# Dealing the second half of the forgetting heads' values out over the first score slots

## The chip, the core and the metric

The kernel runs on one core of a Trainium2 chip. The core has five engines that work side by side, each through its own instructions in order: TensorE (PE in the profile) multiplies matrices and writes the results to PSUM, VectorE (DVE), ScalarE (ACT) and GpSimd (POOL) work on vectors, and SyncE (SP) issues most of the DMA transfers. Engines wait for each other by semaphores. The metric is the device time of one execution in microseconds (us); shorter is better.

## The reference

One decoder layer over a sequence of 1024 tokens, width 1024, in float32. What matters here, cut to its core:

```python
h = rmsnorm(x, ln1[l])
z = h @ w_in[l]
ml_qk, ml_v, ml_o, ml_i, ml_f, fx_q, fx_k, fx_v, fx_f = jnp.split(z, splits, axis=-1)
mh = mlstm_chunkwise(mq, mk, mv, ig, lf)          # 4 heads of 128
...
fx_out = forgetting_attention(fq, fk, fv, flf)    # 8 heads of 64, causal softmax
x = x + jnp.concatenate([ml_out, fx_out], axis=-1) @ w_out[l]
x = x + cross_attention(rmsnorm(x, ln_x[l]), rmsnorm(mem, ln_mem[l]), ...)
u = jax.nn.relu(rmsnorm(x, ln2[l]) @ w_ff1[l])
x = x + (u * u) @ w_ff2[l]
return rmsnorm(x, ln_f)
```

The change concerns `fx_v`: the 1024 x 512 values of the eight forgetting heads, which are a product of the normed tokens with 512 columns of `w_in`. The attention's scores, `fq` times `fk` with the decay added, are computed at the same time.

## The kernel before, in words

Every large product is made of three passes, since the operands are split into a high and a low part (`hi`, `lo`): `mm3` (lines 186 to 188) issues the matmuls low by high, high by low and high by high into one PSUM bank. `split` (lines 134 to 138) makes the parts: ScalarE copies the high part, VectorE subtracts it for the low one.

The values come from `token_major` (line 486). It takes the weight in two halves `c` of 256 columns, four heads each; a half is cut from two weight tiles (`wh`, `wl`, three buffers each) and computed in eight tiles of 128 tokens. A tile is eight `mm3`, 24 matmuls of width 256, in a PSUM bank that `mm()` takes in turn from mm, tp, m2, tp. Then `fv_sink` scales and splits the bank (L137, L138) and stores it to `fvd` in device memory (L652).

The scores go by slots. `slot` (line 1031) takes one step at each stage of the attention: VectorE takes the maxima of the score made one slot ago (L741, L744), ScalarE the exponentials of the one before that (L756), GpSimd scales (L767), and PE makes the next score, a pair of matmuls (L734, L735), into one of three `sc` banks. So a score needs the bank of the third score before it, which is free after that score's exponential. Inside a slot, `in_order` pins each engine's instructions behind the ones pinned before. The first 13 slots (`LEAD_`) only make scores; from then on each slot also transposes probabilities (L782) and multiplies them with values (L801), and fills up with work on the memory tokens, whose operand `hm` is loaded from `hmd` (L1094).

Around these first slots stands the end of the last mLSTM head, `ml_head(3)`, a generator called `closing`. Its first part ends with the row factors `c_fac`: PE sums squares and denominators (L217), VectorE and GpSimd make the factors (L609 to L617, the power on GpSimd at L204). Then it is asked for in steps. The first step transposes `c_fac` on PE into an `sc` bank (L249 in `to_row`), stores it to `facd` and loads it back as a row `r_a` (L251, L253). The second forms the first half of the head's output (L628, L629) and loads the row's second half (L625), the third forms the second half. The buffer `r_a` exists once, so the second load waits for the first L628.

What nobody pins, the framework orders itself: it builds the instructions in the order of the code and then lists them for each engine by its own estimate of when they can start, within the data dependencies and the pins. The banks of a tag are handed out in the order of the code, so in both kernels no score of the slots behind the first closing step stands ahead of that step's transpose. Tiles of the values that are not pinned fall between the slots where that list finds room for them.

Of the kernel before, what the change touches and what calls it, by code (L numbers as in the profile page):

```python
# [44 lines left out]
def hybrid_layer(ctx: ExitStack, tc: tile.TileContext, a: dict, out: bass.AP):  # L45
# [56 lines left out]
    def mm():  # L102

        tag = banks[turn[0] % len(banks)]
        turn[0] += 1
        return ps_tile(tag)
# [36 lines left out]
    @contextmanager  # L143
    def in_order(engines=COMPUTE):

        traced = nc.cur_bb.bb.instructions
        last = traced[-1]
        yield
        start = next(k for k in reversed(range(len(traced))) if traced[k] is last) + 1
        for i in traced[start:]:  # L150
            if i.engine not in engines:
                continue
            if i.engine in last_of:
                tc.add_manual_dep(
                    i,
                    last_of[i.engine],
                    mybir.DependencyInfo(mybir.DependencyClass.NoSync, mybir.DependencyReason.DATA),
                    reason="in_order",
                )
            last_of[i.engine] = i.name  # L160
# [8 lines left out]
    def weights(src, n=1024):  # L169
        return weight_parts(weight_load(src, n))  # L170
# [13 lines left out]
    def mm3(ps, w, x, first, last, more=False):  # L184

        nc.tensor.matmul(ps, w[1], x[0], start=first, stop=False, skip_group_check=more)  # L186
        nc.tensor.matmul(ps, w[0], x[1], start=False, stop=False, skip_group_check=more)  # L187
        nc.tensor.matmul(ps, w[0], x[0], start=False, stop=last, skip_group_check=more)  # L188

    def both(pair, f):  # L190
        return f(pair[0]), f(pair[1])
# [283 lines left out]
    def gate_cols():  # L475
        for dst, src in ((gcol, rel), (emc, steps)):
            tps = ov_()
            for j in range(8):
                nc.tensor.transpose(tps[:, j * MLH : (j + 1) * MLH], src[0:MLH, j * P : (j + 1) * P], ident[:MLH, :MLH])
            s.activation(dst.rearrange("p a b -> p (a b)"), tps[:, : 8 * MLH], AF.Copy if dst is gcol else AF.Exp, scale=1.0 if dst is gcol else -1.0)  # L480
        cut = (w4(dt=F32R)[:GW], w4(dt=F32R)[:GW])
        for sign in range(2):
            split(cut[0], cut[1], cum, 1.0 - 2.0 * sign)
            for p_ in range(2):
                load(decay[sign, p_], cut[p_].bitcast(F32))


    def token_major(w_src, sink, cs=(0, 1), between={}):

        for c in cs:  # L490
            ws = [both(weights(w_src[c, i]), lambda t: t.rearrange("p (k c) -> p k c", k=4)) for i in range(2)]
            for t in range(8):
                if t in between:
                    between[t]()
                hf, tt = divmod(t, 4)
                ps = mm()[:, 0:256]
                for k in range(KT):
                    x = both(h[hf], lambda z: z[:, k, tt * P : (tt + 1) * P])
                    mm3(ps, x, both(ws[k // 4], lambda z: z[:, k % 4]), k == 0, k == KT - 1)
                sink(t, c, ps)  # L500

    def conv_silu(n, hi, lo):
        w = weights(a["w_in"][n])
        z = z4()
        g.memset(z[:, 0:3], 0.0)
        for _, hf, ps in proj(w, h, 1):
            v.tensor_tensor(out=z[:, 3 + hf * TH : 3 + hf * TH + TH], in0=ps, in1=row[:, hf * TH : hf * TH + TH], op=ALU.mult)
        y = z4()[:, :T]
        cw = VEC["conv_w"] + 4 * n
        v.tensor_scalar(out=y, in0=z[:, 0:T], scalar1=vec[:, cw : cw + 1], scalar2=vec[:, VEC["conv_b"] + n : VEC["conv_b"] + n + 1], op0=ALU.mult, op1=ALU.add)  # L510
        for j in range(1, 4):
            v.scalar_tensor_tensor(out=y, in0=z[:, j : j + T], scalar=vec[:, cw + j : cw + j + 1], in1=y, op0=ALU.mult, op1=ALU.add)
        t = z[:, 0:T]
        s.activation(t, y, AF.Tanh, scale=0.5)
        v.scalar_tensor_tensor(out=y, in0=t, scalar=1.0, in1=y, op0=ALU.add, op1=ALU.mult)
        split(hi, lo, y, 0.5)
        return y
# [136 lines left out]
    closing = iter(())  # L654
# [20 lines left out]

    banks[:] = ["tp", "m2", "tp", "sc", "mm", "sc", "sc"]
    turn[0] = 0
    token_major(a["w_mv"], mv_sink, (1,), {2: row_first, 4: gate_rows})
    gate_cols()
    banks[:] = ["mm", "tp", "m2", "tp"]  # L680
    with tc.issue_after(last_sum.ins):
# [2 lines left out]
    for hd in range(MLH):  # L684
        closing = ml_head(hd, *ready)
# [27 lines left out]
    def fx_step():  # L713
        if coming:
            dst, src = coming.pop(0)
            load(dst.bitcast(F32), src)
# [88 lines left out]
    def fx_close(hd, hf, ov):  # L805
        if hd % 2 == 0:
            om[hf] = w2("f")
        rng = slice(hd % 2 * FXD, hd % 2 * FXD + FXD)
        t = w2("c")
        s.activation(t[0:FXD], ov[FXD:], AF.Copy)  # L810
        v.tensor_tensor(out=om[hf][rng], in0=ov[0:FXD], in1=t[0:FXD], op=ALU.add)

    def fx_store(hd, hf):
        if hd == FXH - 1:
            t = w4(dt=F32R)
            mix_fx[hf].append((t[:, :TH], t[:, TH:]))
            split(*mix_fx[hf][-1], om[hf])
            return
        hi, lo = w2("y", dt=F32R), om[hf].bitcast(F32R)
        split(hi, lo, om[hf])  # L820

        def store():
            load(mix[hf, 0, :, MLH + hd // 2], hi.bitcast(F32))
            load(mix[hf, 1, :, MLH + hd // 2], lo.bitcast(F32))

        late.append(store)
# [104 lines left out]
    def mix_step():  # L931
        if pieces:
            dst, src = pieces.pop(0)
            load(dst.bitcast(F32), src)
# [65 lines left out]
    def cut_next():  # L1000

        n, e = divmod(halves[0], 2)
        if n < len(sources) and (e or n < len(raws_) and now[1] - ages[n] >= AGE and sum(u >= now[0] for u, _ in sources[:n]) < 3):
            cut_half()
            return True
# [20 lines left out]
    def slot(values, until):  # L1026
        with in_order((*COMPUTE, mybir.EngineType.SP) if values or until else COMPUTE):
            now[1] += 1
            todo_ = late[:]
            late.clear()  # L1030
            closing = bool(ended)
            ended.clear()
            x = next(steps_, None) if values else None
            if x:
                x.turn()

            while adds and not closing and len(adds) >= (LAG if x else 1):
                y = adds.pop(0)
                y.add()
                if y.last:  # L1040
                    ended.append((y.hd, y.hf, y.ov))
                    break
            tops = scored[:]
            scored.clear()
            for t, e in tops:
                t.top(e)
            if x:
                x.cut()
                adds.append(x)
            exps = topped[:]  # L1050
            topped[:] = tops
            for t, e in exps:
                t.exp(e)
            while exped:
                exped.pop(0).scale()
            exped.extend(t for t, e in exps if e == len(t.parts) - 1)
            for hd, hf, ov in ended:
                fx_close(hd, hf, ov)
                if hd % 2:
                    stores.append((hd, hf, True))  # L1060
            fx_step()
            mix_step()
            part = next(parts, None)
            if part:
                part[0].score(part[1])
                scored.append(part)
            late.extend(filter(None, [f() for f in todo_]))
            if stores and stores[0][2]:
                stores[0] = (*stores[0][:2], False)
            elif stores:  # L1070
                fx_store(*stores.pop(0)[:2])
            while spent[0] < until:
                step = next(fill, None)
                if step is None:
                    break
                spent[0] += step[0]
                if step[1]:
                    late.append(step[2])
                    break
            if until and cut_next() and spent[0] + 6 < until:  # L1080
                cut_next()
        return x
# [2 lines left out]
    fx_load(1)  # L1085
    while coming:
        fx_step()
    for i in range(LEAD_):
        slot(False, 0)
        if i in (1, 11):  # L1090
            next(closing, None)
    token_major(a["w_fv"], fv_sink, between={4: lambda: next(closing, None)})
    hm = act().rearrange("p a b -> p (a b)").rearrange("p (e k c) -> p e k c", e=2, k=KT)
    load(hm.bitcast(F32), hmd)  # L1094
    banks[:] = ["mm", "m2"]
# [752 lines left out]
```

## Time and profile before

| what | value |
|---|---|
| median of 3 runs | 1511.72 us |
| lowest, highest | 1510.87, 1512.04 us |
| profiled execution, span | 1509.2 us |
| median less span | 2.5 us |
| granted TensorE clock, mean | 0.997 |
| PE busy | 1493.0 us (99%) |
| VectorE busy | 1122.7 us (74%) |
| ScalarE busy | 757.7 us (50%) |
| GpSimd busy | 528.7 us (35%) |

The span runs from the first to the last instruction of one profiled execution; its time with what lies around it was not listed apart from the runs. In the rows of a timeline stand the start in us, the duration, the engine, the line, the operation, what it writes and reads, and in brackets the idle time of that engine just before and what ended it. A matmul's duration includes its way through the array; the next one starts before it ends, so the pace is read from the starts. In the table by stretches stand the stretch and its length, then for PE, the weight loads, VectorE, ScalarE and GpSimd the busy time and in brackets the instructions, then the granted clock (1.00 is full), the DMA share and GB/s. The stage of the change lies between about 350 and 400 us.

### The profile page before, as it was taken

How to read it: one execution, taken by the hardware profiler on the slowest of the kernel's cores; microseconds unless marked ns; L12 is line 12 of the kernel's file. 1: busy time of each engine (PE TensorE's matmuls, PEld its weight loads, DVE VectorE, ACT ScalarE, POOL GpSimd, SP SyncE). 2: the span in 40 equal slices, each digit the busy share in tenths (PEclk: the TensorE clock that was granted, in tenths of full speed). 3: DMA queues.
4: the chain of work that ended last, by engine and by line, in shares of the span. 5: the costliest groups of instructions: out<-in, count | busy, mean ns of one | idle time of the engine just before them, and what ended most of it. 6: DMA issues, size and time to landing. Idle time of an engine off the chain costs nothing.

```text
span 1509.2 us, 22358 instructions
## 1 busy us (share of the span) xinstructions
PE 1493.0 (99%) x7806; PEld 1263.7 (84%) x7806; DVE 1122.7 (74%) x1803; ACT 757.7 (50%) x1440; POOL 528.7 (35%) x545
## 2 busy tenths in 40 slices
PE   9999999999999999999999999999999999999997
PEld 9988888889899888788988878888888888888887
DVE  7766676664788875667767899989996678787765
ACT  7324343334688764566654467566664521122134
POOL 1003030414365441623300044454544365553312
PEclk9999999999999999999999999999999999999999
DMA  6322333435777877853354447676678677776623
GB/s 243 115 79 95 98 108 126 132 129 153 247 261 256 284 248 246 271 169 126 128 182 159 147 155 279 235 261 248 217 273 292 264 279 279 279 272 251 247 88 112
DMA packets 124276, 303.04 MB, mean 201 GB/s; under 512 B 13810, under 2 KB 28460, under 8 KB 117252
## 3 DMA queue, kind: packets, MB, share of 16 engines
q1 hardware_dynamic: 124164, 301.62, 57.3%
q8 instruction: 61, 1.00, 0.3%
q14 instruction: 51, 0.42, 0.1%
HBM read 202.75 MB, written 98.82 MB: 200 GB/s over the span
## 4 chain that ended last, share of the span: by engine, by line
PE 90%; DMA 4%; DVE 3%; ACT 1%; issue 1%; POOL 1%; POOLq 0%; DVEq 0%; SPq 0%; ACTq 0%
PE tp L186 8%; PE tp L187 8%; PE tp L188 8%; PE sc L186 6%; PE sc L188 6%; PE sc L187 6%; PE mm L186 5%; PE m L188 5%; PE m L186 5%; PE m L187 5%; PE mm L188 5%; PE mm L187 5%; PE ov L801 2%; PE ov L186 2%; PE ov L187 2%; PE ov L188 2%
## 5 line engine op out<-in xcount | busy, mean ns | idle before, releaser
L186 PE MATMUL tp<-act,wl 128*128 128x512 f32 (+1 forms) x440 | 172.6, 392 | 0.0
L187 PE MATMUL tp<-act,wh 128*128 128x512 f32 (+1 forms) x440 | 172.1, 391 | 0.0
L188 PE MATMUL tp<-act,wh 128*128 128x512 f32 (+1 forms) x440 | 171.8, 392 | 0.0
L135 DVE TENSOR_TENSOR wl<-wr,wh 128x1024 fp32r<-128x1024 f32 (+2 forms) x99 | 131.4, 1327 | 27.0 <-ACT wh L134 26.7
L134 ACT ACTIVATE wh<-wr 128x1024 fp32r<-128x1024 f32 (+2 forms) x99 | 99.8, 1008 | 85.7 <-PE tp L188 32.7
L186 PE MATMUL mm<-act,wl 128*128 128x512 f32 (+1 forms) x332 | 124.8, 376 | 2.6 <-DVE r_c L138 2.1
L188 PE MATMUL mm<-act,wh 128*128 128x512 f32 (+1 forms) x332 | 124.1, 374 | 0.0
L187 PE MATMUL mm<-act,wh 128*128 128x512 f32 (+1 forms) x332 | 123.8, 373 | 0.0
L186 PE MATMUL m<-act,wl 128*128 128x512 f32 (+1 forms) x308 | 113.8, 369 | 0.6 <-DVE wl L135 0.6
L188 PE MATMUL m<-act,wh 128*128 128x512 f32 (+1 forms) x308 | 113.8, 369 | 0.0
L187 PE MATMUL m<-act,wh 128*128 128x512 f32 (+1 forms) x308 | 113.7, 369 | 0.0
L188 PE MATMUL sc<-act,wh 128*128 128x512 f32 (+1 forms) x280 | 105.6, 377 | 0.0
L187 PE MATMUL sc<-act,wh 128*128 128x512 f32 (+1 forms) x280 | 105.6, 377 | 0.0
L186 PE MATMUL sc<-act,wl 128*128 128x512 f32 (+1 forms) x280 | 105.6, 377 | 0.0
L1612 POOL TENSOR_TENSOR z<-wr 128x256 f32<-128x256 f32 x56 | 52.9, 966 | 131.8 <-DMA wr<-w_ff2q 126.7
L188 PEld LDWEIGHTS tp<-act,wh 128*128 128x128 f32 x440 | 82.7, 188 | 19.0
L186 PEld LDWEIGHTS tp<-act,wl 128*128 128x128 f32 x440 | 82.7, 188 | 18.5
L187 PEld LDWEIGHTS tp<-act,wh 128*128 128x128 f32 x440 | 82.7, 188 | 18.2
L134 ACT ACTIVATE wh<-z 128x1024 fp32r<-128x1024 f32 (+1 forms) x54 | 55.5, 1027 | 81.8 <-POOL z L1612 62.3
L135 DVE TENSOR_TENSOR wl<-z,wh 128x1024 fp32r<-128x1024 f32 (+1 forms) x54 | 77.7, 1439 | 11.4 <-ACT wh L134 11.4
L134 ACT ACTIVATE w<-wr 128x768 fp32r<-128x768 f32 (+3 forms) x35 | 28.0, 801 | 107.4 <-PE tp L186 33.0
L186 PEld LDWEIGHTS mm<-act,wl 128*128 128x128 f32 x332 | 62.7, 189 | 14.2 <-DVE r_c L138 2.6
(734 smaller groups left out, 4387.2 us busy)
## 6 DMA issues: line engine op xcount, KB each, us to landing
act<-right SPq DMA_DIRECT2D x49, 1024.0 KB
right<-w SPq DMA_DIRECT2D x56, 256.0 KB
wr<-w_ff2q SPq DMA_DIRECT2D x28, 512.0 KB
right<-r_d SPq DMA_DIRECT2D x49, 256.0 KB
right<-r_e SPq DMA_DIRECT2D x49, 256.0 KB
act<-fqk SPq DMA_DIRECT2D x48, 256.0 KB
wr<-w_in SPq DMA_DIRECT2D x20, 512.0 KB
wr<-w_ff SPq DMA_DIRECT2D x20, 512.0 KB
```

What stands on the lines that cost most here:

```text
L134: s.activation(hi, src, AF.Copy)
L135: return v.tensor_tensor(out=lo, in0=src, in1=hi.bitcast(F32), op=ALU.subtract)
L186: nc.tensor.matmul(ps, w[1], x[0], start=first, stop=False, skip_group_check=more)
L187: nc.tensor.matmul(ps, w[0], x[1], start=False, stop=False, skip_group_check=more)
L188: nc.tensor.matmul(ps, w[0], x[0], start=False, stop=last, skip_group_check=more)
L801: nc.tensor.matmul(self.ov[:, c0:], self.fv[:, self.j], t[:, c0:], start=self.j == 0 and t is self.p[1], stop=self.last and t is self.p[0])
L1612: g.tensor_tensor(out=o, in0=x, in1=y, op=op)
```

## The change

`token_major` becomes a generator that stops after each tile. Its first user, the mLSTM heads' values, runs it to the end as before. The forgetting heads' values are taken apart. The first half (columns 0 to 255, eight tiles) is now written in front of the sixth slot, and is still unpinned. The second half is taken tile by tile, one behind each of the slots six to thirteen, with its PE instructions pinned behind that slot's. Its weight cuts, evictions and stores stay unpinned. The `closing` steps were asked for behind slots 2 and 12 and in each half (the generator has three left, a fourth request does nothing); now behind slot 2, in the first half, and behind slot 12.

```diff
                     mm3(ps, x, both(ws[k // 4], lambda z: z[:, k % 4]), k == 0, k == KT - 1)
                 sink(t, c, ps)
+                yield
...
-    token_major(a["w_mv"], mv_sink, (1,), {2: row_first, 4: gate_rows})
+    for _ in token_major(a["w_mv"], mv_sink, (1,), {2: row_first, 4: gate_rows}):
+        pass
...
+    second_values = token_major(a["w_fv"], fv_sink, (1,))
     for i in range(LEAD_):
+        if i == 5:
+            for _ in token_major(a["w_fv"], fv_sink, (0,), {4: lambda: next(closing, None)}):
+                pass
         slot(False, 0)
         if i in (1, 11):
             next(closing, None)
-    token_major(a["w_fv"], fv_sink, between={4: lambda: next(closing, None)})
+        if i > 4:
+            with in_order((mybir.EngineType.PE,)):
+                next(second_values)
```

Lines behind 501 of the kernel stand one or more lines lower in the changed one (L734 becomes L736, L628 becomes L629); the rows below keep each kernel's own. In the rows, `wh`, `wl` and `act` are the parts of weights and tokens, `tp`, `m`, `mm`, `sc` and `ov` are PSUM banks, each with its number.

The first place is on PE, where the last first-half tile begins. Before:

```order
L186 MATMUL mm_3589<-wh_3579,act_103 128x256
L187 MATMUL mm_3589<-wl_3580,act_102 128x256
L188 MATMUL mm_3589<-wh_3579,act_102 128x256
L249 MATMUL ov_3171<-ident,rcol_m 2x128
L217 MATMUL sc_3146<-ones,r_c_3143 128x1 x4
L186 MATMUL m_560_3519<-wh_3328,act_105 128x256
L187 MATMUL m_560_3519<-wl_3329,act_104 128x256
```

and in the changed kernel:

```order
L186 MATMUL tp_3472<-wh_3256,act_105 128x256
L187 MATMUL tp_3472<-wl_3257,act_104 128x256
L188 MATMUL tp_3472<-wh_3256,act_104 128x256
L249 MATMUL ov_3171<-ident,rcol_m 2x128
L217 MATMUL sc_3146<-ones,r_c_3143 128x1 x4
L186 MATMUL m_541_3443<-wh_3250,act_105 128x256
L187 MATMUL m_541_3443<-wl_3251,act_104 128x256
```

The bank mm_3589 is a tile of the second half; its first twelve matmuls stood ahead of the transpose of `rcol_m` and of the sums L217, and are gone from there.

The second place is on PE too, at the transpose of `c_fac`. Before:

```order
L186 MATMUL tp_3618<-wh_3585,act_103 128x256
L187 MATMUL tp_3618<-wl_3586,act_102 128x256
L188 MATMUL tp_3618<-wh_3585,act_102 128x256
L249 MATMUL sc_3217<-ident,c_fac_2992 8x128
L734 MATMUL sc_3226<-act_3176 128x384
L735 MATMUL sc_3226<-act_3176 128x384
L734 MATMUL sc_3235<-act_3176 128x512
L735 MATMUL sc_3235<-act_3176 128x512
L186 MATMUL tp_3618<-wh_3585,act_103 128x256
L187 MATMUL tp_3618<-wl_3586,act_102 128x256
L188 MATMUL tp_3618<-wh_3585,act_102 128x256
```

and in the changed kernel:

```order
L188 MATMUL m_541_3443<-wh_3256,act_104 128x256
L249 MATMUL sc_3217<-ident,c_fac_2992 8x128
L736 MATMUL sc_3226<-act_3176 128x384
L737 MATMUL sc_3226<-act_3176 128x384
L736 MATMUL sc_3235<-act_3176 128x512
L737 MATMUL sc_3235<-act_3176 128x512
L736 MATMUL sc_3245<-act_3176 128x512
L737 MATMUL sc_3245<-act_3176 128x512
L736 MATMUL sc_3505<-act_3176 128x256
L737 MATMUL sc_3505<-act_3176 128x256
L186 MATMUL mm_3520<-wh_3510,act_103 128x256
L187 MATMUL mm_3520<-wl_3511,act_102 128x256
```

Between the sums and this transpose stood 70 matmuls of tiles, now the 24 of the last first-half tile (m_541). Behind it stand four scores in a row, then a whole tile of the second half (mm_3520), and from there one score and one tile by turns, eight tiles in all. Before, the nine scores behind the first two stood inside tiles, and 134 matmuls of tiles lay between this transpose and the first L782; now it is 192.

The third place is on VectorE, at the closing products. Before:

```order
L628 SCALAR_TENSOR_TENSOR r_f_3062<-r_f_3062,vec,r_a_3216 128x512
L138 SCALAR_TENSOR_TENSOR r_p_3672<-m_574_3647,rcol,r_p_3672 128x4x64
L629 SCALAR_TENSOR_TENSOR r_f_3062<-w_444_2931,r_f_3062 128x512
L741 TENSOR_REDUCE c_mx_3259<-sc_3261 128x1
L138 SCALAR_TENSOR_TENSOR r_c_3701<-tp_3676,rcol,r_c_3701 128x4x64
L138 SCALAR_TENSOR_TENSOR r_f_3062<-r_f_3062,r_y_3306 128x512
L628 SCALAR_TENSOR_TENSOR r_f_2927<-r_f_2927,vec,r_a_3311 128x512
L744 ISA sc_3267,c_mx_3259<-sc_3267,causal,c_mx_3259 128x256
```

and in the changed kernel:

```order
L629 SCALAR_TENSOR_TENSOR r_f_3062<-r_f_3062,vec,r_a_3216 128x512
L743 TENSOR_REDUCE c_mx_3553<-sc_3555 128x1
L138 SCALAR_TENSOR_TENSOR r_c_3545<-mm_3520,rcol,r_c_3545 128x4x64
L630 SCALAR_TENSOR_TENSOR r_f_3062<-w_444_2931,r_f_3062 128x512
L629 SCALAR_TENSOR_TENSOR r_f_2927<-r_f_2927,vec,r_a_3383 128x512
L138 SCALAR_TENSOR_TENSOR r_f_3062<-r_f_3062,r_y_3378 128x512
L746 ISA sc_3590,c_mx_3553<-sc_3590,causal,c_mx_3553 128x256
```

The products still stand among the same slots' maxima. The score sc_3555 follows the first pinned tile, sc_3590 the second. From the transposes L782 of the first values on, and ahead of the first place, the rows of all engines are those of before.

## The prediction

> **What bounds the kernel now.** I read the page first, for the engine that sets the end.
>
> ```profile
> span 1509.2 us, 22358 instructions
> PE 1493.0 (99%) x7806; PEld 1263.7 (84%) x7806; DVE 1122.7 (74%) x1803; ACT 757.7 (50%) x1440; POOL 528.7 (35%) x545
> ```
>
> TensorE (PE) is busy for 1493.0 of 1509.2 us, so only 16.2 us of idle time exist in the whole span. Work that is moved costs nothing by itself; what counts is where PE stands still. Next comes the table by stretches of 10 us over the stage of the change.
>
> ```profile
> 360.00:370.00 10.00, 10.00 (x88) 9.98 (x87) 5.86 (x16) 4.26 (x10) 2.95 (x2) 1.00 0.54 145
> 380.00:390.00 10.00, 8.59 (x66) 8.01 (x66) 8.01 (x23) 5.19 (x15) 2.33 (x4) 1.00 0.88 311
> 390.00:400.00 10.00, 9.01 (x66) 7.96 (x65) 7.49 (x24) 6.90 (x20) 3.91 (x9) 1.00 1.06 366
> ```
>
> The second column is PE's busy time. It misses 1.41 us between 380 and 390 and 0.99 us in the next stretch; between 360 and 370 it misses nothing. Then the timeline of PE, which shows both the stalls and the pace.
>
> ```profile
> 361.62 0.27 PE L249 MATMUL ov<-ident,rcol_m 128*2 128x128 f32 x1
> 361.73 0.95 PE L217 MATMUL sc<-ones,r_c 128*128 128x1 f32 x8
> 362.86 0.28 PE L188 MATMUL m<-wh,act 128*128 128x256 f32 x1
> ...
> 365.45 0.28 PE L186 MATMUL tp<-wh,act 128*128 128x256 f32 x1
> ...
> 370.87 0.27 PE L249 MATMUL sc<-ident,c_fac 128*8 128x128 f32 x1
> 370.89 0.42 PE L734 MATMUL sc<-act 128*128 128x384 f32 x1
> 371.15 0.34 PE L735 MATMUL sc<-act 128*128 128x384 f32 x1
> 371.33 0.40 PE L734 MATMUL sc<-act 128*128 128x512 f32 x1
> 371.56 0.40 PE L735 MATMUL sc<-act 128*128 128x512 f32 x1
> ...
> 381.98 0.44 PE L734 MATMUL sc<-act 128*128 128x384 f32 x1 [0.35 <-ACT act L756]
> 385.44 0.50 PE L734 MATMUL sc<-act 128*128 128x512 f32 x1 [1.07 <-ACT act L756]
> 385.77 0.40 PE L735 MATMUL sc<-act 128*128 128x512 f32 x1
> ...
> 392.80 0.60 PE L782 MATMUL tp<-ident,w 128*128 128x128 f32 x4
> ```
>
> From 362.86 to 365.45, where the next tile begins, lie 22 matmuls of the projection, so one takes 0.118 us and a tile of 24 takes 2.82. A score is a pair; its halves follow each other after 0.23 us at width 512 (371.33, 371.56), 0.18 at 384, 0.12 at 256. What reads 1.07 in brackets costs a little more, since the first matmul behind a stall takes 0.33 instead of 0.23 until the next starts (385.44, 385.77).
>
> **The change part by part.** The work stays the same: as many matmuls, evictions and stores as before. On every engine the rows ahead of the transpose of rcol_m and behind the transposes of the first values (392.80) stand as they did; only the piece between is dealt anew. I price that piece.
>
> *Twelve matmuls leave the place ahead of the denominators' sums.* They were the first half of a second-half tile. At 0.118 us each, L249 of rcol_m and the sums L217 come 1.41 us earlier, and with them the last first-half tile: it is through at 365.45 - 1.41 = 364.04. Its inputs allow it: the square that the sums read left ScalarE before.
>
> *The transpose of c_fac (L249) now has one tile ahead of it where it had nearly three.* It waits for the chain that starts with those sums:
>
> ```profile
> 362.92 0.16 DVE L609 COPY c_sqs<-sc 128x4 f32<-128x4 f32 x1 [1.52 <-ACT c_dens L608]
> 364.33 1.65 POOL L204 TENSOR_TENSOR c_y<-c_var,half 128x8 f32<-128x8 f32 x1 [7.40 <-DVE c_var L198]
> 365.33 1.23 DVE L135 TENSOR_TENSOR wl<-wr,wh 128x1024 fp32r<-128x1024 f32 x1 [1.08 <-ACT wh L134]
> 366.72 1.30 POOL L989 TENSOR_TENSOR wl<-wr,wh 128x512 fp32r<-128x512 f32 x1 [0.74 <-ACT wh L988]
> 366.87 1.18 DVE L206 TENSOR_TENSOR c_t<-c_y 128x8 f32<-128x8 f32 x1
> 368.96 0.17 DVE L617 TENSOR_TENSOR c_fac<-c_fac,c_rd 128x8 f32<-128x8 f32 x1
> 364.24 1.06 ACT L134 ACTIVATE wh<-wr 128x1024 fp32r<-128x1024 f32 x1 [0.98 <-PE m L188]
> ```
>
> c_fac was ready at 368.96 + 0.17 = 369.13, and PE reached its transpose at 370.87: never waited for. The chain is slow because VectorE works in order: the weight cut L135 stands ahead of L206 and waits for ScalarE's wh, which waits for PE (m, L188), and L206 takes 1.18 us beside GpSimd's L989. In the new order these rows stand in the same sequence on VectorE, ScalarE and GpSimd, and each predecessor is 1.41 us earlier. So c_fac comes at 367.72, and with 0.05 for the signal (PE's pair is through at 371.15 + 0.34, VectorE's maximum, below, starts at 371.53) PE starts at 367.8. It has had nothing to do since 364.04: **3.7 us of new stall**, where 70 matmuls stood before. The scores cannot jump ahead, since PE works in order, and the second half's tiles are pinned behind the sixth slot.
>
> *Four scores stand together behind it.* From 367.8 to the third score's end pass 0.92 us (370.87 to 371.79 before, by the rows above) and 0.46. The fourth needs the bank of the first, which is free after the maximum and the exponential:
>
> ```profile
> 371.53 0.57 DVE L744 CUSTOM_DVE_ANT_0 sc<-sc,causal 128x384 f32<-128x384 f32 x1 [0.41 <-PE sc L735]
> 372.19 0.58 ACT L756 ACTIVATE w<-sc,c_mx 128x384 f32<-128x384 f32 x1 [0.74 <-DVE c_den L764]
> 372.66 0.19 ACT L756 ACTIVATION_READ_ACCUMULATOR w<-sc,c_mx 128x1 f32 x1
> ```
>
> 372.66 + 0.19 is 1.98 after the transpose; with the signal 2.03. PE is there at 1.38, so 0.65 us more are lost. The fourth score then ends at 2.37 (0.24 and 0.10 for the restart).
>
> *Then slot and tile alternate.* Eight tiles are 8 x 2.82 = 22.6 us, the seven scores left 4 x 0.46 + 0.36 + 2 x 0.24 = 2.7. If nothing waits, PE reaches the first values' transpose at 367.8 + 2.4 + 22.6 + 2.7, 395.4 with the digits left out here, against 392.80: 2.6 later.
>
> *The old stalls go.* They are in that sum already: before, VectorE stood in front of the two closing products and the maxima behind them came late.
>
> ```profile
> 378.71 0.75 DVE L628 SCALAR_TENSOR_TENSOR r_f<-r_f,vec,r_a 128x512 f32<-128x512 f32 x1 [2.64 <-DMA r_a<-facd]
> 383.57 0.75 DVE L628 SCALAR_TENSOR_TENSOR r_f<-r_f,vec,r_a 128x512 f32<-128x512 f32 x1 [1.52 <-DMA r_a<-facd]
> 373.56 0.33 SPq L253 DMA_DIRECT2D r_a<-facd  x1
> ```
>
> Those cost PE the 0.35 and 1.07 above; with drains and restarts 1.9, since the 21.9 us from 370.87 to 392.80 hold 134 matmuls of tiles (15.8) and eleven scores (4.3). After the change the waits remain, counted from the transpose: the first product at 7.8 (378.71 - 370.87), 5.1 of it from the load's issue at 373.56; the second at 12.7, since its load is issued when the first product ends (379.46) and took 4.1. Queued behind the second on VectorE is the maximum of the score that follows the second pinned tile. The product, one more closing step, the maximum and the exponential, at 0.75 each like the product, make 15.7. The bank so freed is wanted by the score behind the fifth tile: 2.4 + 5 x 2.82 + 1.5 of scores = 18.0. Cover: 2.3 us, so I cost these waits at nothing; without cover they would cost what exceeds it.
>
> *SyncE's queue.* The second half's eight stores and the loads of the third head stand a few places apart from before, the mix stores ahead of hmd's 2 MB instead of behind:
>
> ```profile
> 380.34 0.50 SPq L1094 DMA_DIRECT2D act<-hmd  x1
> 398.89 0.28 PE L186 MATMUL mm<-act,wl 128*128 128x256 f32 x1
> ```
>
> hmd is issued behind the store of the third pinned tile, whose eviction stands some five steps behind the second product: near 385 instead of 380.34. The first key matmul needs it at 398.89 + 2.6 = 401.5, so 16 us remain where 18.5 were: nothing.
>
> Sum without the clock: +2.6 us.
>
> *The clock.* The one long stall of this trace shows what follows one:
>
> ```profile
> 639.20 0.39 PE L188 MATMUL m<-act,wh 128*128 128x512 f32 x1
> 641.74 0.50 PE L186 MATMUL mm<-act,wl 128*128 128x512 f32 x1 [2.14 <-DVE r_c L138]
> 643.45 0.63 PE L188 MATMUL mm<-act,wh 128*128 128x512 f32 x1
> 643.88 0.63 PE L186 MATMUL mm<-act,wl 128*128 128x512 f32 x1
> ...
> 642.00:642.50 0.50, 0.50 (x3) 0.41 (x3) 0.50 (x1) 0.50 (x3) 0.00 (x0) 0.96 0.00 0
> 642.50:643.00 0.50, 0.50 (x2) 0.33 (x2) 0.50 (x2) 0.50 (x2) 0.00 (x0) 0.50 0.39 111
> 645.50:646.00 0.50, 0.50 (x4) 0.41 (x3) 0.05 (x1) 0.42 (x1) 0.00 (x0) 0.62 1.13 377
> ```
>
> After 2.14 us idle the granted clock (the column behind the engines) is 0.50 from 642.48 (0.96: the drop falls at the very end of that half microsecond) to 645.88, and a matmul takes 0.43 us: 3.4 us at half speed, which lose 1.7 us when PE is busy throughout. The stall between 383 and 385 (1.07) kept 1.00. Ours is 3.7, so I expect the drop. Where it falls decides the cost. If the 3.4 us end 2.2 after the transpose, they slow only the first scores, whose extra time fills the 0.65 of waiting and runs over by 0.3. If a second stretch follows, because the first held the stall's end and the 0.65, the four scores end 0.7 late and 2.6 us of tile lose half: 2.0. I take +1.0, between the two.
>
> The Trainium skill ("TensorE: Matmul & The Clock Gate", Part 1: The HAM clock gate) says that the clock halves after a whole idle window of about 3.4 us, the windows running freely. By that rule a 3.7 us stall would seldom hold a whole window and the sum would stay at +2.6. The trace disagrees: 2.14 us were enough. The length of the slow stretch, 3.4 us, agrees.
>
> Total +3.6 us. In the profiled execution's terms the span goes from 1509.2 to 1512.8; the median of the runs, 1511.72, lies 2.5 above that span, which I carry over: **1515.3 us**.
>
> **The rivals.**
>
> *Stall without the drop.* The clock falls only when a window holds more idle time than this split stall leaves in it. For it: 1.07 us did not suffice; the 3.7 us can fall on two windows. Against it: however the 3.7 and the 0.65 fall on stretches of 3.4 us, one of them holds about 2.0 us of idle time, close to the 2.14 that sufficed. Time 1511.72 + 2.6 = 1514.3, within what counts as no change.
>
> *The chain is shorter than before (not slower).* If VectorE's wait for the weight cut and GpSimd's company fall away, the steps behind the 1.65 us power on GpSimd take 4 x 0.17 us, and c_fac is ready at about 366.7 - 1.4 = 365.3. The stall is then 1.3, below what drops the clock: 2.6 - 2.4 = +0.2, 1511.9 us. It decides once c_fac comes within 1.5 us of the last tile. Against it: the same rows stand ahead of L206, and the weight cut cannot run before PE frees its buffer.
>
> *The loads take longer (slower still).* If the two loads of r_a need over 2.3 us more together, the late maximum holds the bank, and from there every microsecond falls on PE. With 2 us beyond the cover: 1517.3. For it: all loads go through one queue, and the values' 0.5 MB stand ahead of the first. Against it: hmd, now behind, no longer competes.
>
> **How the numbers follow.** Forecast 0.58, stall without drop 0.20, short chain 0.12, long loads 0.10. About 0.2% (3.0 us) is what a measurement of this kernel can tell from no change: above 1514.7 is slower, below 1508.7 faster. The forecast with 0.3 to 2.0 for the clock spans 1514.6 to 1516.3, so some four fifths of it count as slower: 0.46, with 0.10 from the loads and 0.02 from the second case 0.58. Faster could come only from the 1.9 us of old stalls, which fall short of 3.0: 0.04. No change 0.38. The range 1511.7 to 1517.2 leaves out the outer parts of the two last cases; the forecast's own is 1514.6 to 1516.3.
>
> **What would show it.** In the changed kernel's PE rows L249 of c_fac carries about 3.6 us of idle time behind VectorE's c_fac, the fourth score about 0.5 behind ScalarE, and no other score between there and L782 (near 395.4) waits. The granted clock reads 0.50 for about 3.4 us near there. I am wrong if that L249 waits less than 1.5 us, if the clock stays at 1.00, or if a score between two tiles waits for an exponential.

## The result, and the profile after

| kernel | median (lowest to highest), us | runs |
|---|---|---|
| before | 1511.86 (1509.72 to 1513.83) | 11 |
| changed | 1515.76 (1513.64 to 1519.10) | 11 |

The ratio is 1.0027, with a 95% interval from 1.0018 to 1.0035: the change costs 3.9 us by the medians, 2.7 to 5.3 by the interval. The forecast was 1515.3.

Whom PE waited for in the stage from 355 to 402 us of the changed kernel (engine, line and what it waited for, total in us, times, longest):

```profile
PE sc L249 <- DVE c_fac L618: 3.5, 1, 3.5
PE tp L784 <- DVE r_b L138: 0.4, 1, 0.4
PE sc L736 <- ACT act L758: 0.2, 1, 0.2
```

The waits in front of the scores, 0.35 and 1.07 us before, are gone. One new wait is larger than both. In PE's timeline of the changed kernel it stands so:

```profile
360.46 0.27 PE L249 MATMUL ov<-ident,rcol_m 128*2 128x128 f32 x1
360.57 0.95 PE L217 MATMUL sc<-ones,r_c 128*128 128x1 f32 x8
...
364.18 0.28 PE L188 MATMUL m<-wh,act 128*128 128x256 f32 x1
367.98 0.38 PE L249 MATMUL sc<-ident,c_fac 128*8 128x128 f32 x1 [3.53 <-DVE c_fac L618]
368.01 0.67 PE L736 MATMUL sc<-act 128*128 128x384 f32 x1
368.48 0.52 PE L737 MATMUL sc<-act 128*128 128x384 f32 x1
...
370.50 0.49 PE L736 MATMUL sc<-act 128*128 128x256 f32 x1
370.80 0.41 PE L737 MATMUL sc<-act 128*128 128x256 f32 x1
371.01 0.41 PE L186 MATMUL mm<-wh,act 128*128 128x256 f32 x1
371.22 0.41 PE L187 MATMUL mm<-wl,act 128*128 128x256 f32 x1
```

The sums end where the forecast had them, the last first-half tile is through at 364.3, and PE then stands until VectorE has `c_fac`. Behind the stall a matmul of width 256 takes 0.21 us until the next starts (371.01, 371.22) where it took 0.118 before. The stretches say why; the column before the last two is the granted clock:

```profile
366.00:366.50 0.50, 0.00 (x0) 0.00 (x0) 0.50 (x1) 0.00 (x1) 0.50 (x1) 0.99 1.18 215
366.50:367.00 0.50, 0.00 (x0) 0.00 (x0) 0.50 (x2) 0.00 (x0) 0.32 (x1) 0.50 0.63 170
373.00:373.50 0.50, 0.50 (x5) 0.50 (x5) 0.00 (x0) 0.00 (x0) 0.00 (x0) 0.69 0.94 385
373.50:374.00 0.50, 0.50 (x7) 0.50 (x6) 0.00 (x0) 0.00 (x0) 0.00 (x0) 1.00 1.01 402
```

The clock is halved from 366.5 to 373.3: 6.8 us, twice the 3.4 us seen before at 642. It falls while PE still waits, and lies over the four scores and the first 2.3 us of the pinned tile.

VectorE's two closing products, and on SyncE's queue (SPq) the stores of the products' high parts `r_y` and the load of `hmd`, in the changed kernel:

```profile
375.35 0.75 DVE L629 SCALAR_TENSOR_TENSOR r_f<-r_f,vec,r_a 128x512 f32<-128x512 f32 x1 [3.33 <-DMA r_a<-facd]
379.41 0.75 DVE L629 SCALAR_TENSOR_TENSOR r_f<-r_f,vec,r_a 128x512 f32<-128x512 f32 x1 [1.72 <-DMA r_a<-facd]
378.38 0.32 SPq L633 DMA_DIRECT2D mix<-r_y  x1
382.75 0.50 SPq L633 DMA_DIRECT2D mix<-r_y  x1
384.83 0.52 SPq L1102 DMA_DIRECT2D act<-hmd  x1
```

VectorE still waits for the two loads (3.33 and 1.72 us), but no score between two pinned tiles waits for VectorE any more. The first transposes of the values come at 397.12 in this execution, 4.3 us later than before; the part ahead of the stage was already 0.2 us late, so the stage itself costs 4.1 here.

The span of this execution is 1514.8 us, 5.6 more than that of the profile before. The rest lies far behind the stage: matched matmul by matmul, the delay falls from 4.2 to 2.2 between 641 and 647 us, grows to 4.1 by 674, and reaches 5.1 at 1189. In a second profile of the changed kernel, below, the delay behind the stage runs another course, so I do not count this part to the change. The section on the hardware takes it up.

### The profile page after: what moved, and what is told of

Its sections match the earlier page's. It is cut to its first block, busy times and chain, and to the rows that moved or that the text cites. A ratio compares the mean times of both kernels' runs of the same rounds, so it can differ in the third digit from the quotient of the medians.

```text
span 1514.8 us, 22359 instructions
## 1 busy us (share of the span) xinstructions
PE 1495.2 (99%) x7806; PEld 1264.7 (83%) x7806; DVE 1120.1 (74%) x1803; ACT 758.4 (50%) x1440; POOL 525.4 (35%) x545
## 4 chain that ended last, share of the span: by engine, by line
PE 87%; DMA 5%; DVE 3%; ACT 2%; POOL 1%; issue 1%; SPq 0%; POOLq 0%; DVEq 0%; ACTq 0%
PE tp L186 8%; PE tp L187 8%; PE tp L188 8%; PE sc L186 6%; PE sc L187 6%; PE sc L188 6%; PE m L188 5%; PE m L187 5%; PE m L186 5%; PE mm L186 5%; PE mm L188 5%; PE mm L187 5%; PE ov L803 2%; PE ov L186 2%; PE ov L187 2%; PE ov L188 2%
## 5 line engine op out<-in xcount | busy, mean ns | idle before, releaser
L186 PE MATMUL tp<-act,wl 128*128 128x512 f32 (+1 forms) x440 | 172.6, 392 | 0.0
L186 PE MATMUL mm<-act,wl 128*128 128x512 f32 (+1 forms) x332 | 124.1, 374 | 2.2 <-DVE r_c L138 1.7
L186 PE MATMUL m<-act,wl 128*128 128x512 f32 (+1 forms) x308 | 113.8, 369 | 0.8 <-DVE wl L135 0.8
L186 PE MATMUL sc<-act,wl 128*128 128x512 f32 (+1 forms) x280 | 105.6, 377 | 0.0
L186 PEld LDWEIGHTS tp<-act,wl 128*128 128x128 f32 x440 | 82.7, 188 | 18.6
L186 PEld LDWEIGHTS mm<-act,wl 128*128 128x128 f32 x332 | 62.4, 188 | 13.8 <-DVE r_c L138 2.1
```

## The experiments

Each ran in several rounds beside the kernel before on the same chip. The medians of the kernel before were 1511.63 (first four runs), 1511.60 (the two with hmd held back) and 1511.79 (the last two).

**The changed kernel once more.** No edit; it stands beside the next three on one chip.

> The changed kernel once more, beside the others on one chip. Theory (PE's wait at the transpose of c_fac, and the halved clock behind it, make the loss): about 1515.8 us, 3.9 above the kernel before. PE's row L249 of c_fac carries 3.5 us of idle time in every profile, but where the slow clock falls differs from execution to execution, so single runs scatter by some 2 us. Rival (a mere shift of work with chance in it): within 1 us of the kernel before.

Measured: 1516.10 us, ratio 1.0031 (1.0019 to 1.0042), so the loss shows again. L249 waits 3.5 us in this profile too. Here the clock is halved for one stretch only:

```profile
368.00:370.00 2.00, 1.77 (x7) 1.44 (x7) 1.05 (x5) 0.70 (x2) 0.35 (x1) 0.68 0.71 248
370.00:372.00 2.00, 2.00 (x10) 1.71 (x9) 1.73 (x8) 1.61 (x6) 1.04 (x3) 0.50 0.13 39
372.00:374.00 2.00, 2.00 (x18) 2.00 (x18) 0.00 (x0) 0.71 (x5) 0.72 (x2) 0.97 0.59 164
```

At the first transposes of the values PE is 3.2 us late (3.73 less the 0.50 that this execution was late ahead of the stage), against 4.1 in the first profile: where the slow stretches fall is worth 0.8 us between two executions of the same kernel.

**Without the pin.**

```diff
         if i > 4:
-            with in_order((mybir.EngineType.PE,)):
-                next(second_values)
+            next(second_values)
```

> The changed kernel without the pin: the second half is still asked for tile by tile behind slots six to thirteen, but PE's list may take its matmuls when it likes. Theory: PE has 70 matmuls of tiles between the sums and the transpose of c_fac again, the 3.5 us wait is gone, the old stalls (0.35 and 1.07 us) are back: 1511.9 us, as before. Rival (moving the first half in front of the sixth slot, or asking for the tiles one by one, makes the loss): stays near 1515.8.

Measured: 1511.57 us, ratio 1.0003 (0.9994 to 1.0012). Twelve matmuls of a second-half tile stand ahead of the sums again and 70 matmuls between the sums and the transpose of `c_fac`, which waits for nothing. So neither the new place of the first half nor the asking tile by tile makes this kernel slower than the one before: the loss comes with the pin, which takes away what filled that gap.

One part of the expectation failed. The old stalls are not back as they were; up to 395 us, PE waits at these two places:

```profile
384.28 0.50 PE L736 MATMUL sc<-act 128*128 128x512 f32 x1 [0.24 <-ACT act L758]
393.57 0.55 PE L784 MATMUL tp<-ident,w 128*128 128x128 f32 x3 [1.05 <-DVE r_b L138]
```

PE reaches the first transposes 1.1 us sooner than in the kernel before (391.69 against 392.80), and more than half of that goes at the second row, where the kernel before waited 0.41. The next experiment shows what stands behind that row.

**The pin kept, the closing steps later.**

```diff
-            for _ in token_major(a["w_fv"], fv_sink, (0,), {4: lambda: next(closing, None)}):
+            for _ in token_major(a["w_fv"], fv_sink, (0,)):
                 pass
         slot(False, 0)
-        if i in (1, 11):
+        if i in (6, 8, 11):
             next(closing, None)
```

> The changed kernel with its pin, but the closing steps are asked for behind the slots 7, 9 and 12 instead of slot 2, the first half and slot 12. So a pinned tile and most of another stand between the last first-half tile and the transpose of c_fac. Theory: the chain to c_fac (6.5 us from the sums) is covered, L249 waits 0, the clock stays at 1.00, and as one tile lies between every two scores the old stalls are gone as well: 1511.9 - 1.9 = 1510.0 us. Rival (the pin itself costs, by scores or evictions that come late in a rigid row): stays above 1513.

Measured: 1511.80 us, ratio 1.0000 (0.9992 to 1.0009). Both sides expected wrongly. L249 waits for nothing and the clock stays at 1.00, and PE reaches the first transposes 1.8 us ahead of the kernel before (390.96 against 392.80), as the theory had it. But the time is that of before. The next thing in PE's timeline takes the gain back:

```profile
390.96 0.60 PE L784 MATMUL tp<-ident,w 128*128 128x128 f32 x4
394.03 0.55 PE L784 MATMUL tp<-ident,w 128*128 128x128 f32 x3 [2.24 <-DVE r_b L138]
```

The second set of transposes of the first values needs the bank of the last tile. VectorE frees it with L138, behind ScalarE's copy, and ScalarE stood still:

```profile
391.62 0.63 ACT L137 ACTIVATE r_y<-r_f 128x512 fp32r<-128x512 f32 x1 [2.77 <-DMA mix<-r_y]
380.45 0.43 SPq L1102 DMA_DIRECT2D act<-hmd  x1
381.47 0.32 SPq L633 DMA_DIRECT2D mix<-r_y  x1
```

The copy `r_y` of the second closing product needs its only buffer, whose store was issued at 381.47, one microsecond behind the 2 MB of `hmd` at 380.45. It was free only at 391.6. In ScalarE's order the eviction of the last tile stands behind this copy. So the wait for `c_fac` is gone, and what the old stalls cost before is now spent in a wait for an eviction. The same copy waited for the same store in the kernel before (1.27 us, at 390.29) and without the pin (3.29 us, at 391.16); before, it did not yet make PE wait longer than the 0.41 that stand there in most runs.

**The idle time filled.**

```diff
                 pass
+            idle = ov_()
+            for _ in range(11):
+                nc.tensor.matmul(idle[:FXD], last_values[6][:, 0, 0], h[0][0][:, 0], start=True, stop=True)
         slot(False, 0)
```

(`last_values`, in lines left out here, collects the evictions of `fv_sink`; its entry 6, the seventh, is that of the tile that PE computes last.)

> The changed kernel with eleven idle matmuls more, 64 x 512 each, that read an eviction of the last first-half tile, write a bank nobody reads and stand in PE's list ahead of the transpose of c_fac. They fill 2.6 of the 3.7 us stall and make nothing later; about 0.8 us of idle time are left. Theory: the transpose comes at the same time as in the changed kernel, but the clock stays at 1.00; the four scores then wait 0.65 us as worked out, and the time falls by the price of the clock alone, 1.0 to 1.8 us: 1514.3 us, 2.4 above the kernel before. Rival (the halved clock hides behind waits and costs nothing): the same 1515.8. Rival (all of the loss is the clock's): 1511.9.

Measured: 1514.76 us, ratio 1.0022 (1.0013 to 1.0031): 3.1 above the kernel before, 1.3 below the changed kernel beside it (1.0 below its first median). The rows of this run:

```profile
365.20 2.71 PE L1100 MATMUL ov<-act,r_b 128*64 128x512 f32 x11 [0.56 <-ACT r_b L137]
368.20 0.27 PE L249 MATMUL sc<-ident,c_fac 128*8 128x128 f32 x1 [0.29 <-DVE c_fac L618]
368.23 0.42 PE L739 MATMUL sc<-act 128*128 128x384 f32 x1
...
370.24 0.39 PE L739 MATMUL sc<-act 128*128 128x256 f32 x1 [0.50 <-ACT w L761]
...
366.00:368.00 2.00, 1.91 (x9) 0.88 (x7) 1.93 (x5) 0.19 (x1) 1.04 (x1) 1.00 0.87 135
368.00:370.00 2.00, 1.55 (x7) 1.03 (x7) 1.29 (x5) 0.75 (x3) 0.38 (x1) 1.00 0.81 288
```

With PE kept at work the clock reads 1.00 throughout, the transpose comes at the same time (368.20; ahead of the stage this execution was 0.2 us later than the changed kernel's first profile), and now the fourth score waits the 0.50 us that the prediction had and the changed kernel did not show, because its scores ran at half speed. At the first transposes PE is 2.4 us late (2.86 less 0.44). So the sum without the clock holds, and the clock's price is about 1.0 to 1.3 us in the medians. The medians' intervals overlap (1.0013 to 1.0031 here, 1.0019 to 1.0042 beside it): that the clock no longer falls is shown by the row, its price only roughly.

**Late steps, and hmd behind the store.**

```diff
-            load(mix[hf, 0, :, hd], yh.bitcast(F32))
+            stored.append(load(mix[hf, 0, :, hd], yh.bitcast(F32)))
...
-    load(hm.bitcast(F32), hmd)
+    with tc.issue_after(stored[6].ins):
+        load(hm.bitcast(F32), hmd)
```

> The kernel with the late closing steps, and the load of hmd (2 MB) held back until the store of the first closing product's high part has been issued. In the run with late steps the old stalls were gone (PE 1.9 us earlier at the last pinned tile), but the first transposes of the values then waited 2.24 us: ScalarE's r_y stood 2.77 us for that store, which lay behind hmd, and the last tile's eviction stood behind r_y. Theory: with the store ahead of hmd that wait falls back to about 0.4, and the time is 1511.8 - 1.8 = 1510.0 us, 1.7 below the kernel before. Rival (the values could not start earlier in any case, something else ends last there): stays within 0.5 of 1511.8, with another name behind the wait. Rival (hmd comes too late for the first key matmul): above 1511.8, with a wait on hmd.

Measured: 1509.34 us, ratio 0.9982 (0.9973 to 0.9991), 2.3 us below the kernel before and over 6 below the changed one. Two rows answer to those of the run with late steps:

```profile
384.90 0.63 ACT L137 ACTIVATE r_y<-r_f 128x512 fp32r<-128x512 f32 x1 [1.92 <-DVE r_f L631]
...
392.59 0.55 PE L785 MATMUL tp<-ident,w 128*128 128x128 f32 x3 [0.41 <-DVE r_b L138]
```

`r_y` waits for its operand and no longer for the store, and the transposes wait 0.41 instead of 2.24 us. No wait on `hmd` appears: PE's waits up to 410 us are the 0.41 here, 0.4 and 0.2. This version beats both kernels. No run holds `hmd` back and leaves the closing steps where they were, so how much of the gain that one edit gives to the kernel before is not shown.

**A dose between.** The same with the closing steps behind the slots 6, 8 and 12 (`i in (5, 7, 11)`).

> The same as the run with hmd held back, but the closing steps behind the slots 6, 8 and 12: then two tiles, 48 matmuls and one score (5.9 us) stand between the sums and the transpose of c_fac instead of 24 matmuls (changed kernel) or 67 and two scores (late steps). A dose between. Theory (the transpose waits for what the chain of 6.5 us leaves uncovered): L249 waits about 0.6 us, too short to halve the clock, and the time is about 1510.6 us, 0.6 above the run with hmd held back. Rival (any wait at this place halves the clock): about 1512.

Measured: 1510.93 us, ratio 0.9996 (0.9987 to 1.0005). L249 waits 0.97 us, more than the 0.6 expected, and the chain itself is longer here (7.87 us from the first sum at 362.81 to the end of `c_fac` at 370.68, against 7.36 in the changed kernel). The granted clock stays at 1.00:

```profile
370.73 0.27 PE L249 MATMUL sc<-ident,c_fac 128*8 128x128 f32 x1 [0.97 <-DVE c_fac L619]
...
366.00:372.00 6.00, 5.03 (x41) 4.74 (x41) 4.63 (x9) 3.11 (x6) 2.93 (x2) 1.00 0.71 183
```

So the wait goes with the cover: 3.5 us with 24 matmuls between the sums and the transpose, 1.0 with 48 and a score, none with 67 and two scores.

**The same without the pin.** The kernel with hmd held back and the steps behind slots 7, 9 and 12, its second half unpinned.

> The run with late closing steps and hmd held back (1509.34 us), but without the pin: the second half's matmuls may stand where PE's list has room. It tells whether the pin adds anything to that version. The list now has one tile and parts of others between most scores by itself. Theory (what counts is that something covers the transpose of c_fac and that scores are spaced; the pin is one way to the spacing): PE waits nowhere between the sums and the first transposes of the values, time within 0.7 us of 1509.34. Rival (only the rigid row of one tile and one score takes the old stalls away): they are back, 1511.2 us.

Measured: 1510.46 us, ratio 0.9991 (0.9982 to 1.0000). PE's waits in the stage are the same three as with the pin (0.4, 0.4 and 0.2 us): the old stalls do not come back, which is against the rival. The time lies 1.1 us above the pinned version, more than the 0.7 allowed, and the intervals overlap. Whether the pin adds anything there stays open.

**The steps close together.** The kernel with hmd held back and `i in (6, 7, 8)`.

> The run with late closing steps and hmd held back, with the closing steps behind the slots 7, 8 and 9 instead of 7, 9 and 12. PE's list is the same up to tile numbers. Theory: the third step's place is free as long as its store's wait is over before the last evictions, so the time is that of the run with hmd held back, 1509.3 us within 0.7. Rival (the steps close together stand in front of the maxima on VectorE): a score waits for an exponential again, above 1510.5.

Measured: 1509.73 us, ratio 0.9987 (0.9978 to 0.9996), PE's waits in the stage again 0.4, 0.4 and 0.2 us. The places of the second and the third step do not matter here, as the theory had it for the third.

## Why the prediction was right, and where not

*The twelve matmuls ahead of the sums.* L249 of `rcol_m` came at 360.46, forecast 360.2; the difference is what this execution was late from its first microseconds on. Right.

*The stall at the transpose of c_fac.* Forecast 3.7 us from tile to transpose, some 3.6 in the brackets; measured 3.53. `c_fac` ended at 367.93, forecast 367.72. That the chain keeps its length because VectorE, ScalarE and GpSimd keep their order held: the sums came 1.16 us earlier than before (360.57 against 361.73) and the end of `c_fac` 1.20 us earlier (367.93 against 369.13), so the steps between them kept their length, and the rival of a shorter chain is out. Without the pin the stall is gone, which shows that it was the missing cover.

*The fourth score.* Forecast: 0.5 us in the brackets behind ScalarE. Not seen in the changed kernel, seen with the clock kept full. The step was right for full speed; at half speed the three scores ahead take longer than the bank.

*The slots behind.* No score between pinned tiles waited; the first load was issued 3.4 us behind the transpose where the forecast had 2.7, but both loads were shorter (4.0 us to the first product instead of 5.1, 3.3 to the second instead of 4.1), so the products came sooner than forecast (7.4 us behind the transpose, forecast 7.8; 11.4, forecast 12.7). The rival of long loads is out. `hmd` was issued at 384.83, forecast near 385, and nothing waited for it.

*The sum without the clock.* Forecast +2.6 us; with the clock kept full, PE was 2.4 late at the first transposes, and the time 3.1 above the kernel before (interval 2.0 to 4.7). Right.

*The clock.* Forecast a drop that costs 1.0 us, between 0.3 and 2.0. It fell in both profiles, for two stretches in one and for one in the other, and kept full it saves 1.0 to 1.3 us in the medians; by the rows it cost 1.7 us in the first (4.1 less the 2.4 with the clock kept full) and 0.8 in the second (3.2 less 2.4), so that the forecast lies this close to the median is partly luck. That a second stretch can follow was in the forecast's upper bound. What was too strong is the reason given: one stall of 2.14 us does not show that 2.14 us suffice (next section but one). The argument against the rival of the stall without the drop, that one stretch of 3.4 us holds about 2.0 us of idle time, held: the stretches that ended with the two falls held 2.04 and 2.93 (the last section shows how they are cut). Two profiles cannot give the rival's frequency.

*The old stalls.* Forecast: worth 1.9 us, and not coming back. In the changed kernel they did not. But in the run with late steps I had expected them to end as a gain at once, and 1.8 of 1.9 us came back as a wait for an eviction. In the changed kernel that wait is missing because both stores of `r_y` are issued ahead of `hmd` (378.38 and 382.75 against 384.83), as the prediction had it; ScalarE's second `r_y` starts at 381.98 and waits for no store. With late steps `hmd` is issued at 380.45, ahead of both. The prediction priced this order only by what `hmd` itself is needed for and did not name the buffer that the stores release.

## What to carry to other kernels

A pin that spaces work evenly also takes it away from the gap that it used to fill: before pinning, look for the chain of small steps on other engines that this work covered, and measure the chain (here 6.5 us from the end of the sums) against the cover that stays (2.8 us). Price the idle time with the clock that follows it, and as a range, since where the slow stretch falls changes from run to run. And when a stall is removed and the time stays, look at the next wait for the same engine: here a 256 KB store behind a 2 MB load held one buffer, and in the kernel with late steps putting the store first gave the gain.

## What the runs showed of the hardware

The stall at the first sum of the residual stage (PE's L186 behind VectorE's r_c, near 641 us before) is in all these kernels, and the clock after it is not decided by its length. Of the profiles, stalls of 0.71, 1.60, 1.70, 2.48, 2.51 and 2.71 us kept the clock at 1.00; stalls of 2.14, 2.2 (two of them) and 2.97 us halved it for a while. The stall of 2.14 us is that of the kernel before, at 641.74, and 0.43 us pass from matmul to matmul behind it; the run without the pin, with 2.48 us, goes on at 0.23.

More can be read from the profiles. The granted clock of the half microsecond in which it changes gives the time of the change: 0.71 for 368.50 to 369.00 means full speed for the first 0.21 us, so it fell at 368.71. That is the second profile of the changed kernel, in which the clock falls once more at 648.61 and is full again at 372.13 and 652.02. From 372.13 to 648.61 pass 276.48 us, 81 times 3.413. In the kernel before, with late steps and with `hmd` held back, 860.16 us pass from the fall at this stall to the one at the end of the run (642.46 to 1502.62 before), 252 times 3.413. So within one execution the clock changes only on a grid of 3.413 us that takes no notice of the stalls. The Trainium skill ("TensorE: Matmul & The Clock Gate", Part 1: The HAM clock gate) says that the window of the clock gate runs freely and gives 3413 ns for it; these profiles agree.

Laid on that grid, the stalls of the stage and of 641 us sort themselves by PE's idle time in a single stretch of it. These are the two closest cases up to 700 us, each with the stretch behind it, first the run with `hmd` held back, then the same without the pin; PE's busy time stands behind the length 3.41:

```profile
636.61:640.02 3.41, 1.48 (x7) 0.86 (x5) 3.08 (x6) 2.09 (x4) 2.89 (x4) 1.00 0.72 268
640.02:643.43 3.41, 3.11 (x7) 2.51 (x8) 3.33 (x5) 2.03 (x4) 0.24 (x1) 0.50 0.51 156
638.25:641.66 3.41, 1.52 (x7) 0.89 (x5) 3.08 (x5) 1.57 (x4) 2.89 (x5) 1.00 0.98 374
641.66:645.07 3.41, 2.60 (x12) 2.15 (x13) 3.33 (x6) 2.55 (x4) 0.76 (x1) 1.00 0.54 163
```

The stretch with 1.93 us of idle time is followed by half speed, the one with 1.89 is not. All six stretches that were followed by a fall held 1.93 to 2.93 us, and none of those with less was. The stall of 2.71 us is the second of these pairs, cut by the grid into 1.89 and 0.81; that of 2.48 us without the pin was cut into 1.21 and 1.27. For the executions in which the clock did not fall here, the grid is carried back from the fall at the end of the run. At that end, where other work runs, the clock fell behind 1.37 and 1.72 us as well, so idle time is not the whole measure. A second slow stretch followed where the first held idle time of its own: 1.49 us in the first profile of the changed kernel and 0.62 with late steps, but not with 0.30 or none.

The Trainium skill, in the same section, has the clock halve after at least one idle window of about 3.4 us. These profiles do not fit that: no stretch ahead of one of these six falls was idle throughout, and in the first profile of the changed kernel the clock fell 2.2 us into the stall of 3.53.

A kept clock is largely given back. Where it stayed full behind that stall, PE waited 0.77 to 1.10 us at 671 to 678 us for VectorE's r_c (1.10 in the first profile of the changed kernel); where it fell for a full stretch (before, the changed kernel's second profile, the run with late steps), there was no wait at that place; in the run with hmd held back, where the slow stretch began within the stall, the wait was 0.66 us. In the first profile of the changed kernel the 2.0 us that it gained on the kernel before around 641 us were lost again by 674 but for less than 0.2. So this does not explain why single executions of one kernel lie up to 5 us apart (1513.64 to 1519.10 for the changed one). The profiles show other waits that come and go: in the second profile of the changed kernel PE waits 1.14 us at 628.25 for VectorE's r_d, and in the first not at all. What makes them come is open, and so is the rest of the difference between the spans (5.6 us) and the medians (3.9).
